# Rotary embedding of an attention block: six VectorE operations over ten heads in place of six for the keys and six for the queries

## The chip, the cores and the metric

The kernel runs on one core of one Trainium2 chip. The core has several engines that run side by side, each working through its own list of instructions in order: PE (TensorE, the matrix multiplier, whose weight loads are shown separately as PEld), DVE (VectorE), ACT (ScalarE), POOL (GpSimd) and SP (SyncE, which here only issues transfers). The metric is the device time of one execution in microseconds (us); lower is better.

## The reference, cut to what matters

The program is a two-layer encoder trunk over 2048 positions of width 1024. The change touches layer 0 only, and in it the attention half: windowed attention with 8 query heads, 2 key/value heads of 64 elements, and a rotary embedding on the first 16 elements of each query and key head.

```python
def partial_rotary(t, positions):
    half = ROPE_DIM // 2                       # ROPE_DIM = HEAD_DIM // 4 = 16
    inv_freq = jnp.power(jnp.float32(ROPE_THETA), -jnp.arange(half, dtype=jnp.float32) / half)
    ang = positions.astype(jnp.float32)[:, :, None, None] * inv_freq
    cos, sin = jnp.cos(ang), jnp.sin(ang)
    tr = t[..., :ROPE_DIM].astype(jnp.float32)
    t1, t2 = tr[..., :half], tr[..., half:]
    rot = jnp.concatenate([t1 * cos - t2 * sin, t2 * cos + t1 * sin], axis=-1)
    return jnp.concatenate([rot.astype(t.dtype), t[..., ROPE_DIM:]], axis=-1)
...
    q = partial_rotary(q.reshape(B, S, N_Q_HEADS, HEAD_DIM), positions)
    k = partial_rotary(k.reshape(B, S, N_KV_HEADS, HEAD_DIM), positions)
    y_attn = windowed_gqa_sink(q, k, v, sink)     # a block of 128 queries sees 3 blocks of 128 keys
```

Per head the rotation is four products of 8 elements, one difference and one sum. Cosine and sine depend on the position only, so that they are the same for all ten heads.

## The kernel before, in words

The sequence is cut into 16 attention blocks of 128 positions. In every tile of the attention stage the 128 positions of a block lie on the 128 partitions. The functions that matter are these.

- `build(u)` (L320) loads and transposes the input of two blocks, scales it and splits it into a high and a low part. It runs once for two blocks, so that the stage has a rhythm of block pairs.
- `project(blk)` (L344) first multiplies keys and values of the block: 24 matmuls with 256 columns into the PSUM bank `pk` (L351). Then it multiplies the queries: 24 matmuls with 512 columns into the bank `pq` (L355). The matmuls stand in the helper `mm3` (L158 to L160). ACT copies the keys (L358), the values (L361) and the queries (L362) out of PSUM; keys and queries go into one tile `qk` of ten heads, the queries in heads 0 to 7 and the keys in heads 8 and 9. Then come the rotary operations on DVE (L371 to L376), first for heads 8 to 10, then for heads 0 to 8, with the scratch tile `rot`.
- Still in `project`, the rotated keys are split for the matmul: ACT writes the high part (L380), DVE the low part (L381), PE transposes both (four transposes, L385), and ACT copies the result to its place in `kT` (L393; some blocks have two places).
- `scores(blk)` (L399) splits the rotated queries (`split`, L154 on ACT and L155 on DVE), transposes them on PE (L420), copies them (L421), multiplies them with the keys of up to three blocks (L428, L429), masks and takes the row extreme on DVE (L430), the exponential on ACT (L433), scales the rows on DVE (L440) and transposes the result in pieces of 32 by 32 on DVE (L458, two long instructions in a row). Transfers (L465) put the pieces in place.
- `values(blk)` (L469) multiplies with the values (L475) and stores the block.

The calls stand in this order: `project(0)`, `project(1)`, `scores(0)`, `project(2)`, and then for each block `blk`: `scores(blk + 1)`, for even blocks `build((blk + 4) // 2)`, `values(blk)`, `project(blk + 3)`. So `scores(n)` needs the keys of block n + 1, which are projected just ahead of it in this order. Near the end of the stage the first matmuls of the next one (the spatial gate, L549) are interleaved.

The order in which each engine runs its instructions is not written by hand. A planner places the program's instructions when the kernel is built: it steps through its own estimate of time, takes on each engine the instruction of highest priority (priority follows the order of the calls) that its estimate shows as ready, and writes that order down. On the chip every engine then follows its list in order and waits where an operand is not there yet. `qk` has four buffers, `rot` two, and the PSUM banks used for the projections (`pj`) two, for transposes (`px`) two and for the scores (`psc`) three.

Of the kernel before, what the change touches and what calls it, by code (L numbers as in the profile page):

```python
# [11 lines left out]
ALU = mybir.AluOpType  # L12
# [41 lines left out]
def kernel(  # L54
# [29 lines left out]
    tt = nc.vector.tensor_tensor  # L84
# [9 lines left out]
    def pool(stack, name, side=None, bufs=1, space=None):  # L94
        kw = {} if space is None else {"space": space}
        if side is not None:
            kw["side"] = side
        return stack.enter_context(tc.tile_pool(name=name, bufs=bufs, reuse_waits="tile", **kw))
# [58 lines left out]
    def mm3(ps, ahi, alo, bhi, blo, first, last):  # L157
        nc.tensor.matmul(ps, lhsT=ahi, rhs=bhi, start=first, stop=False)  # L158
        nc.tensor.matmul(ps, lhsT=ahi, rhs=blo, start=False, stop=False)  # L159
        nc.tensor.matmul(ps, lhsT=alo, rhs=bhi, start=False, stop=last)  # L160

    def bank(p, tag, shape=(128, C)):
        t = p.tile(list(shape), F32, tag=tag, name=tag)
        return t
# [99 lines left out]
    cos_t = ap.tile([128, 16, 8], F32, name="cos_t")  # L264
    sin_t = ap.tile([128, 16, 8], F32, name="sin_t")
# [43 lines left out]
    def k_place(n, p):  # L309
        if n not in kTs:  # L310
            kTs[n] = ap.tile([128, 4, 768], F32R, tag="kT", bufs=2, name="kT")
        return kTs[n][:, :, p * 128:p * 128 + 128]
# [31 lines left out]
    def project(blk):  # L344
        if blk >= NB:
            return
        hT = hTs[blk // 2]
        sl = slice(blk % 2 * 128, blk % 2 * 128 + 128)
        pk = bank(pj, "pj")
        for k in range(KD):  # L350
            mm3(pk[:, 0:256], hT[0][k][:, sl], hT[1][k][:, sl], wqh[:, k, 512:768], wql[:, k, 512:768], k == 0,  # L351
                k == KD - 1)
        pq = bank(pj, "pj")
        for k in range(KD):
            mm3(pq, hT[0][k][:, sl], hT[1][k][:, sl], wqh[:, k, 0:512], wql[:, k, 0:512], k == 0, k == KD - 1)  # L355
        qk = ap.tile([128, 10, 64], F32, tag="qk", bufs=4, name="qk")
        qkb[blk] = qk
        act(out=qk[:, 8:10, :], in_=pk[:, 0:128].rearrange("p (h d) -> p h d", h=2), func=AF.Copy)  # L358
        vt = ap.tile([128, 128], F32, tag="vt", bufs=7, name="vt")
        vts[blk] = vt  # L360
        act(out=vt, in_=pk[:, 128:256], func=AF.Copy)  # L361
        act(out=qk[:, 0:8, :], in_=pq.rearrange("p (h d) -> p h d", h=8), func=AF.Copy)  # L362
        rot = ap.tile([128, 4, 10, 8], F32, tag="rot", bufs=2, name="rot")
        for h0, h1 in ((8, 10), (0, 8)):
            n = h1 - h0
            cb = cos_t[:, blk:blk + 1, :].to_broadcast([128, n, 8])
            sb_ = sin_t[:, blk:blk + 1, :].to_broadcast([128, n, 8])
            t1 = qk[:, h0:h1, 0:8]
            t2 = qk[:, h0:h1, 8:16]
            r0, r1, r2, r3 = (rot[:, i, h0:h1, :] for i in range(4))  # L370
            tt(out=r0, in0=t1, in1=cb, op=ALU.mult)  # L371
            tt(out=r1, in0=t2, in1=sb_, op=ALU.mult)
            tt(out=r2, in0=t2, in1=cb, op=ALU.mult)
            tt(out=r3, in0=t1, in1=sb_, op=ALU.mult)
            tt(out=t1, in0=r0, in1=r1, op=ALU.subtract)
            tt(out=t2, in0=r2, in1=r3, op=ALU.add)  # L376
        ks = ap.tile([128, 4, 128], F32R, tag="ks", bufs=2, name="ks")
        kf = qk[:, 8:10, :]
        kd = ks[:, 0:2, :].rearrange("p k (u d) -> p k u d", u=2)
        act(out=kd, in_=kf[:, :, None, :].to_broadcast([128, 2, 2, 64]), func=AF.Copy)  # L380
        tt(out=ks[:, 2:4, :].rearrange("p k (u d) -> p k u d", u=2),  # L381
           in0=kf[:, :, None, :].to_broadcast([128, 2, 2, 64]), in1=kd.bitcast(F32), op=ALU.subtract)
        ps = bank(px, "px")
        for i in range(4):
            nc.tensor.transpose(ps[:, i * 128:i * 128 + 128].bitcast(F32R), ks[:, i, :], ident_r)  # L385
        n, p = divmod(blk, 4)
        places = [(n, p + 1)]
        if p == 0 and n > 0:
            places.insert(0, (n - 1, 5))
        if p == 3 and blk < NB - 1:  # L390
            places.append((n + 1, 0))
        for place in places:
            act(out=k_place(*place), in_=ps.rearrange("p (i n) -> p i n", i=4), func=AF.Copy)  # L393
# [108 lines left out]
    tq = pool(sb, "shuf", right)  # L502
    tail = []
    project(0)
    project(1)
    scores(0)
    project(2)
    for blk in range(NB):
        scores(blk + 1)
# [142 lines left out]
    for i in range(4):  # L652
        stt(out=bias_sg[:, i, :], in0=ps[:, i * 128:i * 128 + 128], scalar=vcol0[:, 52 + i:53 + i],
            in1=bias_sg[:, i, :], op0=ALU.mult, op1=ALU.add)
# [485 lines left out]
    op = pool(ctx, "outp", right)  # L1140
# [86 lines left out]
```

## Time and profile before

| what | value |
|---|---|
| time, median of 3 runs | 1574.51 us (1571.71 to 1579.4) |
| the profiled execution's own time | 1574.79 us |
| its span, first to last instruction | 1573.0 us |
| mean granted TensorE clock | 0.984 |
| PE busy | 1480.3 us, 94% of the span |
| PEld busy | 1184.1 us, 75% |
| DVE busy | 1187.1 us, 75% |
| ACT busy | 783.3 us, 50% |
| POOL busy | 385.2 us, 24% |
| first and last rotary operation (start) | 52.0 and 280.5 us |

How to read the rows that are quoted below. A row of the timeline has the start in us, the length in us, the engine, the line of the kernel, the operation, the tile written and the tiles read, the shape, and how many instructions are merged in the row; brackets at the end show idle time ahead of it and what ended that. A row of the groups has the number of instructions, their busy time in us, the mean of one in ns, and the idle time ahead of them. Two instructions in a row on one engine overlap a little in such rows, so that the distance between two starts says more of the cost than the length. PEclk is the share of full speed that was granted to the TensorE clock. A busy PE includes modelled ends of matmuls.

### The profile page before, as it was taken

The page shows a single profiled execution, that of the slowest core. Times are in us where ns is not written, and L with a number is a line of the kernel's source. Part 1 is how long each engine was busy: PE and PEld are TensorE (multiplying, and loading weights), DVE is VectorE, ACT ScalarE, POOL GpSimd, SP SyncE. Part 2 cuts the span into 40 slices and gives each one's busy share as a digit, 9 for nine tenths or more (in the row PEclk, how much of TensorE's full clock was granted, in tenths as well). Part 3 has the DMA queues.
Part 4 walks back from the last instruction along what each step waited for, and adds up shares of the span by engine and source line. Part 5 has one row for each costly group of instructions (what it writes and reads, how often), then busy time and mean ns, then how long its engine had stood idle before and what let it go on. Part 6 is the DMA issues. An engine that isn't in the chain of part 4 may idle for free. (4 is left out here: it accounts for less than half of the span.)

```text
span 1573.0 us, 22049 instructions
## 1 busy us (share of the span) xinstructions
PE 1480.3 (94%) x7096; PEld 1184.1 (75%) x7096; DVE 1187.1 (75%) x2180; ACT 783.3 (50%) x1470; POOL 385.2 (24%) x464
## 2 busy tenths in 40 slices
PE   6899999899999999999999899999999999868997
PEld 3787777557877777788887688788778788757886
DVE  4499889745769558966866775987987687788985
ACT  4677767543423332343243228499489496841100
POOL 1023232002004000300120232634634532133231
PEclk9999999899999999999999999999999999989999
DMA  9367776749798989988785699887877676369751
GB/s 346 124 173 217 220 199 183 236 141 297 239 291 303 253 257 293 314 272 261 263 292 180 190 262 278 239 255 281 224 243 269 220 230 221 119 198 344 253 194 54
DMA packets 210747, 370.91 MB, mean 236 GB/s; under 512 B 56616, under 2 KB 105924, under 8 KB 210632
## 3 DMA queue, kind: packets, MB, share of 16 engines
q1 hardware_dynamic: 205032, 356.89, 71.3%
q0 software_dynamic: 5600, 12.62, 3.0%
q8 instruction: 56, 0.92, 0.2%
q14 instruction: 59, 0.48, 0.1%
HBM read 261.96 MB, written 85.97 MB: 221 GB/s over the span
## 5 line engine op out<-in xcount | busy, mean ns | idle before, releaser
L154 ACT ACTIVATE hl<-raw 128x512 fp32r<-128x512 f32 x192 | 118.6, 627 | 215.4 <-DMA raw<-in_ev_w_in_dram 131.8
L159 PE MATMUL pj<-alo,hl 128*128 128x512 f32 x512 | 201.1, 393 | 0.0
L158 PE MATMUL pj<-ahi,hl 128*128 128x512 f32 x512 | 200.1, 393 | 1.1 <-DVE gz L753 1.1
L160 PE MATMUL pj<-ahi,hl 128*128 128x512 f32 x512 | 200.1, 392 | 0.0
L155 DVE TENSOR_TENSOR hl<-raw,hl 128x512 fp32r<-128x512 f32 x192 | 132.0, 698 | 63.1 <-ACT hl L154 62.7
L150 POOL TENSOR_SCALAR rstd<-mv 128x1 f32<-128x1 f32 x32 | 31.1, 972 | 415.3 <-DVE mv L616 303.6
L158 PEld LDWEIGHTS pj<-ahi,hl 128*128 128x128 f32 x512 | 96.8, 189 | 22.0 <-DVE gz L753 1.5
L159 PEld LDWEIGHTS pj<-alo,hl 128*128 128x128 f32 x512 | 96.9, 189 | 20.4
L160 PEld LDWEIGHTS pj<-ahi,hl 128*128 128x128 f32 x512 | 96.6, 189 | 20.2
L430 DVE CUSTOM_DVE_ANT_0 P<-psc,mask,nsink 128x384 f32<-128x384 f32 (+1 forms) x128 | 73.8, 596 | 24.0 <-PE psc L429 23.9
L158 PE MATMUL pj<-wqh,hhi 128*128 128x256 f32 (+1 forms) x256 | 87.9, 347 | 2.5 <-ACT hhi L154 1.7
L154 ACT ACTIVATE phl<-praw 128x512 fp32r<-128x512 f32 x56 | 35.3, 631 | 107.1 <-DMA praw<-in_od_w_in_dram 55.8
L159 PE MATMUL pj<-wql,hhi 128*128 128x256 f32 (+1 forms) x256 | 87.4, 342 | 0.0
L160 PE MATMUL pj<-wqh,hlo 128*128 128x512 f32 (+1 forms) x256 | 85.2, 345 | 1.4 <-DVE hlo L155 1.4
L977 DVE SCALAR_TENSOR_TENSOR ii<-ii,xc 128x1024 f32<-128x1024 f32 (+2 forms) x32 | 40.7, 1272 | 59.0 <-ACT ii L971 59.0
L433 ACT ACTIVATE P<-P,nm 128x384 f32<-128x384 f32 (+1 forms) x128 | 76.4, 601 | 16.4 <-DVE nm L430 15.8
L465 POOL DMA_DIRECT2D P<-T x88 | 48.8, 562 | 143.9 <-DVE nm L430 79.0
L777 POOL TENSOR_TENSOR alo<-hm,ahi 128x512 fp32r<-128x512 f32 x32 | 50.3, 1578 | 118.8 <-DVE hm L776 102.2
L947 DVE SCALAR_TENSOR_TENSOR xc<-X,vcol,xc 128x512 f32<-128x512 f32 (+2 forms) x96 | 77.7, 845 | 0.3
L158 PE MATMUL pm<-xhi,hg 128*128 128x512 f32 (+3 forms) x160 | 56.0, 364 | 14.3 <-ACT xhi L154 6.3
L155 DVE TENSOR_TENSOR phl<-praw,phl 128x512 fp32r<-128x512 f32 x56 | 39.2, 700 | 35.2 <-ACT phl L154 31.9
L966 ACT ACTIVATE ra<-pm,vcol 128x512 f32<-128x512 f32 (+2 forms) x80 | 47.2, 604 | 29.6 <-PE pm L160 29.3
(304 smaller groups left out, 4288.7 us busy)
## 6 DMA issues: line engine op xcount, KB each, us to landing
hl<-w_d SPq DMA_DIRECT2D x128, 512.0 KB, 4.8
raw<-in_ev_w_in_dram SPq DMA_DIRECT2D x128, 256.0 KB, 4.1
w_d<-phl SPq DMA_DIRECT2D x40, 512.0 KB, 4.7
aw<-in_ada_w_dram SPq DMA_DIRECT2D x32, 512.0 KB, 6.8
hg<-w_d SPq DMA_DIRECT2D x32, 512.0 KB, 4.2
P<-T SPq DMA_DIRECT2D x128, 96.0 KB, 3.8
aw<-in_ada_w_dram SPq DMA_DIRECT2D x8, 1024.0 KB, 7.7
xp<-in_x_dram SPq DMA_DIRECT2D x32, 256.0 KB, 3.3
```

Of the source, the lines that this page charges most:

```text
L154: act(out=hi, in_=src, func=AF.Copy)
L155: tt(out=lo, in0=src, in1=hi.bitcast(F32), op=ALU.subtract)
L158: nc.tensor.matmul(ps, lhsT=ahi, rhs=bhi, start=first, stop=False)
L159: nc.tensor.matmul(ps, lhsT=ahi, rhs=blo, start=False, stop=False)
L160: nc.tensor.matmul(ps, lhsT=alo, rhs=bhi, start=False, stop=last)
L430: nc.vector.tensor_tensor_reduce(out=p[:, g, 0:W], in0=ps[:, 0:W], in1=mask[:, m0:m0 + W], scale=-0.125, scalar=nsink[:, h:h + 1], op0=ALU ...
L433: act(out=p[:, g, 0:W], in_=p[:, g, 0:W], func=AF.Exp, scale=-1.0, bias=nm[:, h:h + 1], accum_out=rs[:, h:h + 1])
L465: dma.dma_start(out=pv[32 * r:32 * r + 32, 0:nb, i], in_=T[32 * i:32 * i + 32, 0:nk].rearrange("p (j r) m -> p r j m", r=4)[:, r])
L777: nc.gpsimd.tensor_tensor(out=lo[:, j], in0=h, in1=hi[:, j].bitcast(F32), op=ALU.subtract)
L947: stt(out=xc[:, w], in0=xt[:, j0 + j:j0 + j + W], scalar=vcol1[:, 8 * j + g:8 * j + g + 1], in1=xc[:, w], op0=ALU.mult, op1=ALU.add)
L966: r = act(out=ra[i][:, e, p0:p0 + n], in_=p[:, 0:n], func=AF.Sigmoid, bias=vcol1[:, 40 + q:41 + q])
L977: stt(out=ii[i][:, :, w], in0=ii[i][:, :, w], scalar=1.0, in1=xc[:, None, w].to_broadcast([128, 2, W]), op0=ALU.add, op1=ALU.mult)
```

## The change

In `project` the loop over the two groups of heads goes away. The six operations (four products, a difference, a sum) are issued once for a block, over all ten heads, where six were issued for the two key heads and six for the eight query heads. The tiles, their buffers and all else stay. The first of the six now needs both the copy of the keys (L358) and the copy of the queries (L362), and the keys are rotated by the same instructions as the queries.

```diff
         rot = ap.tile([128, 4, 10, 8], F32, tag="rot", bufs=2, name="rot")
-        for h0, h1 in ((8, 10), (0, 8)):
-            n = h1 - h0
-            cb = cos_t[:, blk:blk + 1, :].to_broadcast([128, n, 8])
-            sb_ = sin_t[:, blk:blk + 1, :].to_broadcast([128, n, 8])
-            t1 = qk[:, h0:h1, 0:8]
-            t2 = qk[:, h0:h1, 8:16]
-            r0, r1, r2, r3 = (rot[:, i, h0:h1, :] for i in range(4))
-            tt(out=r0, in0=t1, in1=cb, op=ALU.mult)
-            tt(out=r1, in0=t2, in1=sb_, op=ALU.mult)
-            tt(out=r2, in0=t2, in1=cb, op=ALU.mult)
-            tt(out=r3, in0=t1, in1=sb_, op=ALU.mult)
-            tt(out=t1, in0=r0, in1=r1, op=ALU.subtract)
-            tt(out=t2, in0=r2, in1=r3, op=ALU.add)
+        cb = cos_t[:, blk:blk + 1, :].to_broadcast([128, 10, 8])
+        sb_ = sin_t[:, blk:blk + 1, :].to_broadcast([128, 10, 8])
+        t1 = qk[:, :, 0:8]
+        t2 = qk[:, :, 8:16]
+        r0, r1, r2, r3 = (rot[:, i] for i in range(4))
+        tt(out=r0, in0=t1, in1=cb, op=ALU.mult)
+        tt(out=r1, in0=t2, in1=sb_, op=ALU.mult)
+        tt(out=r2, in0=t2, in1=cb, op=ALU.mult)
+        tt(out=r3, in0=t1, in1=sb_, op=ALU.mult)
+        tt(out=t1, in0=r0, in1=r1, op=ALU.subtract)
+        tt(out=t2, in0=r2, in1=r3, op=ALU.add)
```

## The prediction

> **What bounds the kernel now.** I read the page first, then the busy times of three stretches of the attention stage, then PE's waits there. The page names PE as the busiest engine by far.
>
> ```profile
> span 1573.0 us, 22049 instructions
> PE 1480.3 (94%) x7096; PEld 1184.1 (75%) x7096; DVE 1187.1 (75%) x2180; ACT 783.3 (50%) x1470; POOL 385.2 (24%) x464
> ```
>
> An average says little of one stage. The rotary operations start between 52.0 and 280.5 us, so the stretches that count are the steady part of the attention stage and its end. The first row below is five block pairs long, from one copy of a first block's queries (L362) to the fifth one after it; the columns are length, then busy time of each engine.
>
> ```profile
> core 0: us, PE busy (x) PEld busy (x) DVE busy (x) ACT busy (x) POOL busy (x), PEclk, DMA share, GB/s
> 97.58:262.63 165.05, 162.07 (x957) 126.79 (x956) 148.12 (x488) 122.67 (x347) 51.91 (x90) 1.00 0.72 200
> 75.00:275.00 200.00, 197.03 (x1167) 156.39 (x1166) 180.79 (x611) 148.83 (x422) 57.02 (x99) 1.00 0.70 195
> 275.00:350.00 75.00, 66.41 (x291) 43.36 (x290) 43.83 (x125) 35.07 (x92) 3.68 (x6) 0.93 0.62 186
> ```
>
> In the steady part a pair of blocks takes 165.05 / 5 = 33.0 us. PE is idle for 165.05 - 162.07 = 2.98 us of the five pairs, 0.6 us a pair. DVE is busy for 148.12 / 165.05 = 90%: high, but with 17 us of room. The waits of PE between 75 and 275 us (line that waited, releaser, us in total, times, longest) say what the little idle time is:
>
> ```profile
> PE pj L160 <- DVE hlo L155: 1.4, 1, 1.4
> PE po L475 <- issue: 0.8, 3, 0.3
> PE px L331 <- DMA xp<-in_x_dram: 0.7, 1, 0.7
> ```
>
> None waits for a rotated key or query; one of 1.4 us waits for DVE at all. The stage is bound by PE, and the operations that change stand on an engine beside it.
>
> **The change part by part.** First what goes and what grows on DVE. These are groups between 50 and 285 us, the first and the last of the six lines in both shapes (16 elements a partition for the keys, 64 for the queries); the other four lines lie between them within 7 ns.
>
> ```profile
> L371 DVE TENSOR_TENSOR rot<-qk,cos_t 128x64 f32<-128x64 f32 x16 | 3.5, 218 | 4.2 <-ACT qk L362 4.2
> L376 DVE TENSOR_TENSOR qk<-rot 128x64 f32<-128x64 f32 x16 | 3.5, 221 | 0.0
> L371 DVE TENSOR_TENSOR rot<-qk,cos_t 128x16 f32<-128x16 f32 x16 | 2.7, 171 | 2.8 <-ACT qk L358 2.8
> L376 DVE TENSOR_TENSOR qk<-rot 128x16 f32<-128x16 f32 x16 | 2.7, 170 | 0.0
> ```
>
> Next, one first block of a pair as the timeline shows it; all rows that the steps need stand here once.
>
> ```profile
> 129.41 0.17 DVE L371 TENSOR_TENSOR rot<-qk,cos_t 128x16 f32<-128x16 f32 x1
> 129.50 0.17 DVE L372 TENSOR_TENSOR rot<-qk,sin_t 128x16 f32<-128x16 f32 x1
> 129.65 0.59 ACT L362 ACTIVATE qk<-pj 128x512 f32<-128x512 f32 x1
> 130.93 0.17 DVE L376 TENSOR_TENSOR qk<-rot 128x16 f32<-128x16 f32 x1
> 131.36 3.43 DVE L458 STREAM_TRANSPOSE T<-P 128x1536 f32<-128x1536 f32 x2
> 131.93 0.41 ACT L380 ACTIVATE ks<-qk 128x256 fp32r<-128x256 f32 x1
> 135.49 0.42 DVE L381 TENSOR_TENSOR ks<-qk,ks 128x256 fp32r<-128x256 f32 x1
> 136.37 0.22 DVE L376 TENSOR_TENSOR qk<-rot 128x64 f32<-128x64 f32 x1
> 140.07 0.29 PE L385 MATMUL px<-ident_r,ks 128*128 128x128 f32 x2
> 140.40 0.60 ACT L393 ACTIVATE kT<-px 128x512 fp32r<-128x512 f32 x1 [0.55 <-PE px L385]
> 143.31 0.41 PE L428 MATMUL psc<-kT,qT 128*128 128x384 f32 x1
> ```
>
> *Removed:* 6 x 16 = 96 operations of the small shape. One costs the queue the distance of two starts, 129.50 - 129.41 = 0.09 us, so 0.54 us a block; as busy time they are 6 x 2.7 = 16.2 us.
>
> *Grown:* 96 operations go from 64 to 80 elements, a size that the trace does not show. From 16 to 64 elements one grows by (220 - 170) / 48 = 1.04 ns an element, so 16 more elements cost 17 ns: 0.10 us a block, 1.6 us in all. The lower bound is nothing, the upper one the whole small operation (0.09 us). I take 17 ns, a straight line just beyond its end.
>
> *Net on DVE:* -0.54 + 0.10 = -0.44 us a block, 16 x 0.44 = 7.0 us of queue time over the stage (by busy time 16.2 - 1.6 = 14.6 us, too much, since neighbours overlap). *Worth at the end:* PE is what sets the pace, and DVE's relief can only fill PE's idle time: at most 2.97 us between 75 and 275 us, of which 1.4 us waits for DVE. I take a gain of 0.5 us; the bounds are 0 and 3.
>
> *Moved: the keys.* Their rotation now waits for the query copy (L362), and in DVE's list it takes the place of the queries' six operations or one near it. What is queued behind: the ACT split (L380), the DVE split (L381), the four transposes (L385), the copy (L393), and the scores that use the new keys.
>
> In the first block of a pair the two copies come close together; what matters is the last of the six operations. The keys were ready at 130.93 + 0.17 = 131.10 us, and would be at 136.37 + 0.22 = 136.59 us, 5.49 us later. But L381 sat behind the two 32x32 transposes (L458) until 135.49 anyway and ended at 135.91. After the change it ends at 136.59 + 0.41 + 0.42 = 137.42, 1.51 us later. The second transposes of the keys ran at 140.07, so that 2.65 us are still in hand there; and if all behind L381 slid by the whole 1.51 us, the copy would end at 140.40 + 0.60 + 1.51 = 142.51, ahead of the scores at 143.31. Cost 0, with 0.80 us of cover in the worse reading. Without the cover each microsecond costs PE a microsecond.
>
> In the second block of the pair the query copy comes ten microseconds behind the key copy, so that the delay is large, and so is the cover:
>
> ```profile
> 139.88 0.43 DVE L381 TENSOR_TENSOR ks<-qk,ks 128x256 fp32r<-128x256 f32 x1 [0.48 <-ACT ks L380]
> 146.90 0.22 DVE L376 TENSOR_TENSOR qk<-rot 128x64 f32<-128x64 f32 x1
> 147.03 3.43 DVE L458 STREAM_TRANSPOSE T<-P 128x1536 f32<-128x1536 f32 x2
> 155.08 0.45 PE L385 MATMUL px<-ident_r,ks 128*128 128x128 f32 x4
> ```
>
> The keys would be ready at 147.12 and, even with L381 put behind the transposes, split at 147.03 + 3.43 + 0.42 = 150.88; PE takes them at 155.08. Cover 4.2 us, cost 0. The PE list loses nothing in between: the keys' transposes stood there after the queries' matmuls already.
>
> At both ends of the stage the cover is thinner:
>
> ```profile
> 62.75 0.22 DVE L376 TENSOR_TENSOR qk<-rot 128x64 f32<-128x64 f32 x1
> 66.21 0.28 PE L428 MATMUL psc<-kT,qT 128*128 128x256 f32 x1
> 280.53 0.22 DVE L376 TENSOR_TENSOR qk<-rot 128x64 f32<-128x64 f32 x1
> 281.81 3.43 DVE L458 STREAM_TRANSPOSE T<-P 128x1536 f32<-128x1536 f32 x2
> 284.39 0.34 PE L428 MATMUL psc<-kT,qT 128*128 128x384 f32 x1
> 287.43 1.19 PE L158 MATMUL pja<-hl,ahi 128*128 128x512 f32 x2 [2.52 <-DMA ahi<-h_d]
> 290.58 0.63 PE L160 MATMUL pja<-hl,alo 128*128 128x512 f32 x1
> 291.01 0.63 PE L159 MATMUL pja<-hl,ahi 128*128 128x512 f32 x1
> 293.55 0.39 PE L160 MATMUL px<-hl,alo 128*128 128x512 f32 x1
> 293.78 0.40 PE L158 MATMUL px<-hl,ahi 128*128 128x512 f32 x1
> ```
>
> At the start: 62.97 + 0.41 + 0.42 + 0.45 + 0.60 = 64.85, ahead of the first scores at 66.21. Cost 0. At the end: block 15's keys ready at 280.75, split by 281.58 if L381 goes ahead of the transposes, cost 0; if behind, 281.81 + 3.43 + 0.42 + 0.45 + 0.60 = 286.71 in place of the 284.39 at which the scores of block 14 want them. PE then waits for a transfer until 287.43 anyway, so that most of the 2.3 us is hidden. I take 0, with 2.3 as the upper bound.
>
> *Sum,* against the profiled execution's own 1574.79 us (span 1573.0, 1.8 us outside it; 0.3 us above the median of the runs shown): 1574.8 - 0.5 + 0 + 0 + 0 = 1574.3, call it **1574 us**.
>
> The rule that speaks against the change is in the Trainium skill, "Perfetto Trace Analysis", section "Optimizing Scalar/DVE Operations": grouping into larger operations pays where the engine is saturated, and where it is not but causes bubbles elsewhere, breaking instructions up may let work end sooner. At 90% DVE is between the two; by this rule the merged six would be the wrong way for the keys, which is the first rival below. By its first half the sum would be the 1568 of the second rival, by its second half the 1597 of the first. No run here shows the merged form yet; the trace of the split one shows PE without a bubble behind the keys.
>
> **The rivals.**
>
> *Slower: PE waits for the keys in each pair.* The place is the first block of a pair. If the copy of the keys slides by the whole 5.49 us (L381 behind one more burst on DVE), it ends at 141.00 + 5.49 = 146.49, 3.18 us past the scores at 143.31; 7 pairs give 22 us, 1597 us. It decides from the point where L381 ends later than 135.91 + 2.31 = 138.22. For it: the cover is under 3 us. Against: 0.80 us are left in the worse reading, and the planner can put other matmuls first. A stall can also cost twice: after the wait of 2.52 us the starts lie 0.43 us apart until 293.55, then 0.23, so PE ran at about half speed for some 6 us and lost 2.9 us more.
>
> The Trainium skill, "TensorE: Matmul & The Clock Gate", section "Why this matters for your kernels", has the clock drop after gaps over about 3 us. By that rule the stall of 3.18 us is just long enough, and by the row above shorter ones are.
>
> *Faster: DVE sets the pace after all.* PE's busy time holds modelled ends, and PEld is busy for only 126.79 / 165.05 = 77%. Then the whole relief shows: 1574.8 - 7.0 = 1568, or by busy time 1574.8 - 14.6 = 1560. Against it: PE's waits name DVE for 1.4 us in 200.
>
> *The planner writes a different order.* New estimated lengths can move ties anywhere behind the change. The work stays the same; what can move are PE's waits, 1573.0 - 1480.3 = 92.7 us over the span, the largest of them near the end of layer 1:
>
> ```profile
> PE pj L158 <- DMA wo<-wo_d: 17.6, 1, 17.6
> ```
>
> A part of one such wait, up or down, is about 10 us: 1565 or 1585.
>
> **How the numbers follow.** Forecast 0.54. Keys late 0.13, all of it slower. DVE sets the pace 0.13, of it 0.10 faster by more than 0.5%. Another order 0.20: 0.08 faster, 0.07 slower, 0.05 neither. 0.5% is 7.9 us, about what a measurement of this kernel can tell from no change. So faster 0.18, within 0.54 + 0.03 + 0.05 = 0.62, slower 0.20. The likeliest case's own range is 1570 to 1579 (gain to 3, loss to 2.3, and the spread of the runs shown). The range for 8 in 10 goes to 1562, inside the faster rival, and to 1588, between the replanned order and the rival with late keys; beyond lie about 0.08 on either side.
>
> **What the profile after would show.** Right: 96 rotary operations of about 237 ns and none of the small shape; a pair still 33 us long with PE idle for about 0.6 us of it; DVE busy some 14 us less between 50 and 285 us; L381 later, L385 and L428 at their old distances. Wrong: waits of PE (L385, L428) on L381 or on the copy L393, pairs 2 us longer and a lower granted clock (slower rival); pairs shorter by 1 us with DVE as full as before (faster rival); equal pairs but waits moved behind 350 us (another order). A rotary operation over 100 ns longer than I take it would break the sum on DVE.

## The result, and the profile after

The kernel after takes 1586.83 us, median of 4 runs (1584.96 to 1588.39), against 1573.43 us, median of 4 runs of the kernel before in the same comparison. The ratio is 1.0068, 95% interval 1.0047 to 1.0089: slower by 13.4 us. The forecast was 1574.0 us, no change.

The page of the profiled execution after (1584.96 us): the span and the busy time of each engine.

```profile
span 1583.3 us, 21941 instructions
PE 1488.5 (94%) x7096; PEld 1185.2 (75%) x7096; DVE 1179.2 (74%) x2084; ACT 784.9 (50%) x1470; POOL 388.6 (25%) x464
```

The span has grown by 10.3 us. DVE lost 96 instructions and 1187.1 - 1179.2 = 7.9 us of busy time, close to the 7.0 us of queue time that the prediction took off. The groups of the kernel after (mean length of one in ns) show the new size near the estimate of 237 ns:

```profile
L369 DVE TENSOR_TENSOR rot<-qk,cos_t 128x80 f32<-128x80 f32 x16 | 3.8, 235 | 14.0 <-ACT qk L362 14.0
...
L374 DVE TENSOR_TENSOR qk<-rot 128x80 f32<-128x80 f32 x16 | 3.7, 231 | 0.0
```

So the change does on DVE what it says. The time is lost elsewhere. The start of each block's query copy (L362) tells where, read from the timelines of both kernels:

| query copy of block | 0 | 2 | 3 | 4 | 6 | 8 | 10 | 12 | 14 | 15 |
|---|---|---|---|---|---|---|---|---|---|---|
| before, us | 52.04 | 71.45 | 85.69 | 97.58 | 129.65 | 162.42 | 195.74 | 227.13 | 262.63 | 276.31 |
| after, us | 51.69 | 69.98 | 80.89 | 101.19 | 139.35 | 171.75 | 203.56 | 237.46 | 274.61 | 289.42 |
| later by | -0.4 | -1.5 | -4.8 | 3.6 | 9.7 | 9.3 | 7.8 | 10.3 | 12.0 | 13.1 |

Almost all of it is lost once, between blocks 3 and 6; from there to block 12 a pair takes (237.46 - 139.35) / 3 = 32.7 us, where it took (227.13 - 129.65) / 3 = 32.5 us. Another 2.8 us go between blocks 12 and 15. The busy times by stretch, first of the kernel before, then of the one after (length, then busy time of each engine, the granted clock behind the engines):

```profile
75.00:100.00 25.00, 25.00 (x160) 22.63 (x158) 23.11 (x86) 21.30 (x63) 4.38 (x8) 1.00 0.56 170
100.00:125.00 25.00, 24.71 (x143) 18.49 (x142) 23.36 (x78) 19.06 (x53) 10.51 (x18) 1.00 0.66 182
125.00:150.00 25.00, 25.00 (x147) 19.09 (x146) 21.75 (x73) 17.01 (x49) 5.55 (x10) 1.00 0.69 188
...
150.00:250.00 100.00, 98.67 (x583) 76.97 (x581) 89.11 (x299) 74.71 (x211) 30.96 (x55) 1.00 0.75 209
```

```profile
75.00:100.00 25.00, 22.21 (x137) 18.92 (x136) 21.11 (x74) 21.25 (x64) 4.52 (x8) 1.00 0.40 121
100.00:125.00 25.00, 21.87 (x117) 15.96 (x117) 19.06 (x62) 17.91 (x54) 5.30 (x9) 0.89 0.58 164
125.00:150.00 25.00, 25.00 (x144) 19.31 (x141) 21.51 (x62) 13.80 (x40) 10.06 (x17) 0.97 0.66 189
...
150.00:250.00 100.00, 98.47 (x584) 76.42 (x583) 84.57 (x250) 73.40 (x203) 30.21 (x53) 1.00 0.71 203
```

Between 75 and 150 us PE was busy for 74.71 us before and is for 69.08 us after: 5.6 us more idle time. The clock takes up to 25 x 0.11 + 25 x 0.03 = 3.5 us more, an estimate from above, since it also counts a low clock while PE was idle. Together that is up to 9.1 us, near the 9.7 by which block 6 is late. From 150 to 250 us the two kernels are alike.

What PE waits for in that stretch of the kernel after (line, releaser, us in total, times, longest):

```profile
PE px L331 <- ACT P L431: 3.0, 1, 3.0
PE px L331 <- DMA xp<-in_x_dram: 1.6, 1, 1.6
PE pj L158 <- ACT hhi L154: 0.6, 1, 0.6
```

No row names a key. PE's longest waits stand ahead of the transposes of the next block pair's input (`build`, L331). The timeline of the kernel after shows how the start has moved; matmuls of the projections between these rows are left out.

```profile
60.91 0.60 ACT L362 ACTIVATE qk<-pj 128x512 f32<-128x512 f32 x1 [0.85 <-PE pj L160]
...
61.54 0.24 DVE L369 TENSOR_TENSOR rot<-qk,cos_t 128x80 f32<-128x80 f32 x1 [5.96 <-ACT qk L362]
...
63.21 0.43 DVE L379 TENSOR_TENSOR ks<-qk,ks 128x256 fp32r<-128x256 f32 x1 [0.54 <-ACT ks L378]
...
67.69 0.46 PE L383 MATMUL px<-ident_r,ks 128*128 128x128 f32 x4
...
71.88 0.35 PE L426 MATMUL psc<-kT,qT 128*128 128x256 f32 x1
...
108.01 1.94 PE L473 MATMUL po<-P,vt 128*64 128x512 f32 x8
...
115.13 0.60 PE L331 MATMUL px<-ident,xp 128*128 128x128 f32 x4
...
116.11 6.00 SPq L325 DMA_DIRECT2D xp<-in_x_dram  x3
...
120.62 1.09 PE L331 MATMUL px<-ident,xp 128*128 128x128 f32 x4 [3.00 <-ACT P L431]
...
122.28 4.84 PE L473 MATMUL po<-P,vt 128*64 128x512 f32 x12
```

Block 1's keys wait for the query copy at 60.91, are split at 63.64, and PE takes them only at 67.69, without a wait of its own: its list has projection matmuls ahead of them. In the kernel before the same two steps were:

```profile
57.27 0.43 DVE L381 TENSOR_TENSOR ks<-qk,ks 128x256 fp32r<-128x256 f32 x1 [0.84 <-ACT ks L380]
...
61.12 0.45 PE L385 MATMUL px<-ident_r,ks 128*128 128x128 f32 x4
```

There the transposes stood 61.12 - 57.70 = 3.42 us behind the split; in the kernel after it is 67.69 - 63.64 = 4.05 us. The distance went along with the keys. It did so in first blocks of a pair, too: in block 6 the last transposes stood 4.16 us behind the split and stand 4.03 us behind it. In second blocks it did not: there the distance was long, 13.8 us in block 5 and 14.8 us in block 7, and shrank to 3.3 and 1.4 us.

The first scores are 5.67 us late (71.88 for 66.21). PE does projections ahead in the meantime (block 3's query copy is 4.8 us early), and I take it that what it has done ahead it lacks later. The first values come at 108.01 in place of 100.68. At 120.62 PE resumes after 3.00 us of waiting. The row names ACT, but these transposes read no `P`. What they need, I take it, is a load that could be issued only once the transposes at 115.13 had freed one of two input buffers, at 115.73; it was issued at 116.11, and loads in this stretch landed 3.8 us after their issue, at about 120. In the kernel before, twelve value matmuls (113.60 us) stand in PE's list between two such groups of transposes (111.49 and 116.78 us); here they stand behind the wait, at 122.28.

### The profile page after: what moved, and what is told of

Its sections match the earlier page's. It is cut to its first block, busy times and chain, and to the rows that moved or that the text cites. A ratio compares the mean times of both kernels' runs of the same rounds, so it can differ in the third digit from the quotient of the medians.

```text
span 1583.3 us, 21941 instructions
## 1 busy us (share of the span) xinstructions
PE 1488.5 (94%) x7096; PEld 1185.2 (75%) x7096; DVE 1179.2 (74%) x2084; ACT 784.9 (50%) x1470; POOL 388.6 (25%) x464
## 5 line engine op out<-in xcount | busy, mean ns | idle before, releaser
L158 PE MATMUL pj<-wqh,hhi 128*128 128x512 f32 (+1 forms) x256 | 87.6, 346 | 3.1 <-ACT hhi L154 2.3
L159 PE MATMUL pj<-wql,hhi 128*128 128x512 f32 (+1 forms) x256 | 87.2, 341 | 0.0
L775 POOL TENSOR_TENSOR alo<-hm,ahi 128x512 fp32r<-128x512 f32 x32 | 49.7, 1562 | 117.9 <-DVE hm L774 113.9
```

What stands on the lines that cost most here:

```text
L775: nc.gpsimd.tensor_tensor(out=lo[:, j], in0=h, in1=hi[:, j].bitcast(F32), op=ALU.subtract)
```

## The experiments

Two theories were told apart first. One: the keys' wait for the query copy costs the time, wherever it comes from. The other: what decides is the count and size of DVE's operations, or simply that the planner wrote another order. Ratios are to the kernel before, measured side by side, with 95% intervals.

**The wait and the operations, one without the other.** Four kernels. The first keeps twelve operations a block, but puts one query head into the keys' group, so that the keys need the query copy:

```diff
-        for h0, h1 in ((8, 10), (0, 8)):
+        for h0, h1 in ((7, 10), (0, 7)):
```

> Twelve operations in two groups as before, but the first group is heads 7 to 10 and the second heads 0 to 7: elements and number of operations stay, and the keys now need the query copy, as after. Theory 'start' and rival 'every pair' both: the wait for the query copy is the cause, 1582 to 1590 us. If the merged operation itself (its size, or six fewer instructions in the planner's estimate) were the cause, this would be at 1572 to 1577 us.

The second has six operations a block and no wait: keys apart, three operations for a group over all 16 rotated elements of a head, with tables of cosine and signed sine made once by four small POOL operations (`cb` and `sb_` are 16 wide here, `r1v` is `r1` in two halves). It was measured twice.

```diff
+        for h0, h1 in ((8, 10), (0, 8)):
...
+            t = qk[:, h0:h1, 0:16]
+            tt(out=r0, in0=t, in1=cb, op=ALU.mult)
+            tt(out=r1, in0=t, in1=sb_, op=ALU.mult)
+            tt(out=t.rearrange("p h (u d) -> p h u d", u=2), in0=r0.rearrange("p h (u d) -> p h u d", u=2),
+               in1=r1v[:, :, ::-1, :], op=ALU.add)
```

> Keys first and queries after them as before, but each group in three operations over 16 elements a head (product with cosine twice over, product with sine of both signs, sum with the halves exchanged): six operations a block as after, without the wait for the query copy. Four small POOL operations are added once to lay out the tables. Theories 'start' and 'every pair': no loss, 1570 to 1575 us; relief of DVE brings at most 1 to 3 us since PE sets the pace. If fewer operations were harmful in themselves: 1580 us or more.

> The kernel with the keys apart and three operations of 16 elements a head for each group, once more and with more rounds: six operations a block, as in the kernel after, and no wait of the keys for the query copy. Theory that late keys cost the time: 0.994 to 0.999 of before, as the first time. Theory that each new order of the planner is a draw of plus or minus 0.4% and the first result was a lucky one: the same order gives the same time, so that this can only tell whether 0.997 was noise of the measurement; then 0.999 to 1.002.

The last has the same three operations over all ten heads, three a block, with the wait:

```diff
-        for h0, h1 in ((8, 10), (0, 8)):
+        for h0, h1 in ((0, 10),):
```

> The same three operations, but over all ten heads, so three operations a block and keys that wait for the query copy: the fewest operations of all kernels here. Theory that the count of operations on VectorE sets the time: at most 0.997. Theory that late keys cost the time: 1.003 to 1.008, although DVE has the least to do.

| kernel | operations a block | keys wait | ratio |
|---|---|---|---|
| before | 12 | no | 1 |
| one query head with the keys | 12 | yes | 1.0118 (1.0077 to 1.0160) |
| after | 6 | yes | 1.0068 (1.0047 to 1.0089) |
| three operations a group | 6 | no | 0.9970 (0.9946 to 0.9994), again 0.9977 (0.9957 to 0.9996) |
| three operations, all heads | 3 | yes | 1.0077 (1.0056 to 1.0098) |

The wait alone makes the kernel slower by 1.2% (1594.82 us, above the 1582 to 1590 expected), and with the three operations it is the whole difference between 0.9977 and 1.0077. With early keys half as many operations buy 0.2 to 0.3%, and once the keys are late a second halving buys nothing. By wait is meant here that the keys' operations name the query copy as an input: the planner sees it too and writes another order, and these runs don't part the two. Groups of the two kernels with three operations, the one without the wait first (its line numbers are 377 to 379):

```profile
L377 DVE TENSOR_TENSOR rot<-qk,cos 128x128 f32<-128x128 f32 x16 | 4.6, 286 | 4.9 <-ACT qk L368 4.8
...
L377 DVE TENSOR_TENSOR rot<-qk,cos 128x32 f32<-128x32 f32 x16 | 3.0, 186 | 3.3 <-ACT qk L364 3.2
```

```profile
L377 DVE TENSOR_TENSOR rot<-qk,cos 128x160 f32<-128x160 f32 x16 | 5.1, 321 | 20.9 <-ACT qk L368 20.9
```

DVE has the least to do in the merged one, but it stands idle for 20.9 us ahead of the first operation, where it was 4.9 + 3.3 us. Their stretch from 75 to 150 us, without the wait and then with it:

```profile
75.00:150.00 75.00, 73.56 (x439) 59.35 (x439) 66.53 (x206) 58.55 (x164) 20.02 (x35) 1.00 0.65 183
```

```profile
75.00:150.00 75.00, 68.76 (x408) 55.17 (x407) 61.25 (x184) 53.54 (x159) 20.31 (x35) 1.00 0.60 170
```

PE is busy for 73.56 - 68.76 = 4.8 us less with the wait, much as in the kernel after (5.6 us). The kernel with keys apart and three operations beats both kernels: before by 0.2 to 0.3%, after by about 1%.

**Where the loss is made.** Five kernels use the merged form for some blocks and the split form for the others; the first one, split for blocks 0 to 2, stands for all:

```diff
-        cb = cos_t[:, blk:blk + 1, :].to_broadcast([128, 10, 8])
+        for h0, h1 in ((8, 10), (0, 8)) if blk < 3 else ((0, 10),):
```

> Blocks 0 to 2 are rotated in two groups (keys first) as before, blocks 3 to 15 in one group as after. Theory 'start': the loss is made where the first scores wait for the keys of block 1 (first score matmul at 66.21 us before, 71.88 us after); it comes back here, so 1573 to 1577 us, and the first score matmul at about 66 us. Rival 'every pair': 13 of 16 blocks still have late keys, so about 1583 to 1587 us. Rival 'another order': neither; any time between 1570 and 1590, with waits in places that neither names.

> The reverse: blocks 0 to 2 in one group as after, blocks 3 to 15 in two groups as before. Theory 'start': nearly the whole loss, 1582 to 1588 us, first score matmul at about 72 us. Rival 'every pair': three blocks of sixteen, 1574 to 1577 us. The two kernels together should add up to the whole loss of 13 us if either theory holds; if they do not, the order that the planner writes has a share of its own.

> Two groups in blocks 0 to 7, one group from block 8 on. Theory 'slip': the query copies of blocks 0 to 7 at the times of before, a loss of about 10 us within the two pairs after block 8, 1583 to 1590 us. Rival 'start only': 1573 to 1578 us. Rival 'a cost for each late block': about 1580 us.

> One group in the even blocks only, the first of each pair, whose key and query copies lie 0.9 us apart in the trace of before. Theory 'slip by the wait for the query copy': little to lose, 1572 to 1580 us. If the order that the planner writes suffers from any merged block: 1585 us or more.

> One group in the odd blocks only, the second of each pair, whose query copy lies 6 to 11 us behind the key copy (from 104.02 to 110.28 us, from 133.33 to 143.22). Theory 'slip': the whole loss, 1583 to 1592 us, with PE idle and a lower granted clock between 75 and 150 us. If the 4.2 us of cover that the prediction counted there were real: 1573 to 1578 us.

| merged in | ratio | query copy later than before, at block 4, 6, 8, 10, 14 (us) |
|---|---|---|
| blocks 3 to 15 | 1.0061 (1.0041 to 1.0081) | -1.0, 4.8, 8.7, 9.0, 9.3 |
| blocks 0 to 2 | 1.0086 (1.0056 to 1.0117) | 3.8, 8.4, 8.7, 8.4, 8.4 |
| blocks 8 to 15 | 1.0090 (1.0069 to 1.0110) | -0.3, -0.2, -0.2, 10.3, 18.9 |
| even blocks | 1.0113 (1.0087 to 1.0140) | 5.1, 5.0, 13.6, 17.9, 26.6 |
| odd blocks | 1.0073 (1.0047 to 1.0099) | 5.8, 8.8, 6.7, 10.6, 14.9 |

This struck down the thought that the thin cover at the start was the only cause: with the start split again some 9 us are lost all the same, about a pair further on. The first two kernels lose 0.61% and 0.86%, together about twice the 0.68% of the change, so that, as their expectation has it, the order that the planner writes has a share of its own. It struck down a cost for each late block, too: three merged blocks cost as much as sixteen. In the first three kernels of the table the loss is a slip, made within some blocks behind the point where keys turn from early to late. With three merged blocks the copy of block 6 stands at 138.07 us and that of block 14 at 271.07, exactly the 133.0 us of the kernel before: thirteen blocks with early keys behind it give nothing back, since PE has next to no idle time in which to catch up (98.49 of the 100 us from 150 to 250 us are busy).

The lateness of a copy shows where time goes in one traced execution, and not what the kernel loses as a whole: two kernels below, with early keys and another order (priority on the keys' chain), stand 6.1 and 8.0 us late at block 14, and their ratios are 1.0026 and 1.0004. (Their traced executions took 1584.54 and 1580.40 us, above their medians of 1578.76 and 1577.22.)

Even blocks alone, whose query copy comes about a microsecond behind the key copy, cost more than odd ones. Their expectation gave them little to lose if the length of that wait set the price, and 1585 us or more if any merged block upset the order; they took 1595.47 us, so the length of the wait doesn't set the price. Nor does the number of turns from early to late keys: both kernels turn late in each pair, and cost less than the kernel below whose pairs alternate (1.0200, four turns). Both also hold a block of the start (0, or 1), so that neither tries its place in the pair by itself.

In the kernel that turns late at block 8 the slip is seen directly. Its timeline, first the row of PE, then SP's issues ahead of it:

```profile
181.23 0.66 PE L331 MATMUL px<-ident,xp 128*128 128x128 f32 x4
...
197.32 1.09 PE L331 MATMUL px<-ident,xp 128*128 128x128 f32 x4 [6.42 <-DMA xp<-in_x_dram]
```

```profile
178.60 0.38 SPq L325 DMA_DIRECT2D xp<-in_x_dram  x1
...
181.69 7.45 SPq L465 DMA_DIRECT2D P<-T  x8
...
193.07 5.73 SPq L325 DMA_DIRECT2D xp<-in_x_dram  x3
```

The transposes at 181.23 had freed a buffer at 181.89, but the next loads of `build` stand in SP's list behind eight transfers of `P` and five stores, until 193.07: eleven microseconds with a free buffer and no load. PE is idle for 6.42 us.

**Is it the late loads?** The largest loss came where pairs of blocks alternate between the two forms, and its waits of PE between 75 and 350 us are mostly for input loads:

```diff
+        for h0, h1 in ((0, 10),) if blk // 2 % 2 == 1 else ((8, 10), (0, 8)):
```

> Blocks 2, 3, 6, 7, 10, 11, 14, 15 in one group, the others in two: the keys turn late four times. Theory 'slip' (PE loses its lead once, each time that the keys turn from early to late, some 10 us, and a saturated PE never gets it back): more than the change itself, 1595 to 1615 us. Rival 'a cost for each late block': half the loss of the change, about 1580 us. Rival 'one slip for all': like the change, 1585 to 1590 us.

```profile
PE px L331 <- DMA xp<-in_x_dram: 16.9, 9, 4.4
```

Two ways to free the loads were tried on it, each with a control on the kernel before: issue them on ACT, which has no eight transfers in its list, or give `xp` a third buffer, so that they can be issued earlier.

```diff
-            load(out=xp, in_=xs[u * 256:u * 256 + 256, k2 * 256:k2 * 256 + 256].rearrange("(b p) f -> p b f", p=128))
+            nc.scalar.dma_start(out=xp, in_=xs[u * 256:u * 256 + 256, k2 * 256:k2 * 256 + 256].rearrange("(b p) f -> p b f", p=128))
```

```diff
-            xp = jp.tile([128, 2, 256], F32, tag="xp", bufs=2, name="xp")
+            xp = jp.tile([128, 2, 256], F32, tag="xp", bufs=3, name="xp")
```

> The alternating kernel (keys late in blocks 2, 3, 6, 7, 10, 11, 14, 15; 31 us over before), with the input loads of build (L325) issued from ACT's list in place of SP's. Theory 'load behind the transfers': PE's waits there are for input loads that the planner put behind eight transposed pieces (L465, some 0.9 us of issue each) in SP's list; with the loads out of that list most of the loss goes, 1575 to 1590 us, and no wait of PE on xp over 1 us. Rival 'keys': PE waits because the scores come late, whatever the load does; 1600 us or more, with waits under another name.

> Control: the kernel before with its input loads issued from ACT's list. Both theories: within 5 us of before, 1572 to 1582 us, since before has only 0.7 us of waits for these loads between 75 and 275 us; a load that waits for PE can hold ACT's list up, which would add some us.

> The alternating kernel with three buffers in place of two for the input tile of build, loads on SP as before, so that a load need not wait for PE to free the tile before. Theory 'load behind the transfers': part of the loss goes, 1580 to 1600 us. Rival 'keys': 1603 to 1612 us as with two buffers.

> The kernel before with a third buffer for the input of the block pairs: the control of the two runs with three such buffers (alternating 1.0047, after 1.0088). Theory that late loads behind the transfers make the alternating kernel's extra loss: the control stands at 0.998 to 1.002, so that the alternating kernel has kept only what late keys cost once. Theory that the buffer merely moves the planner's order: the control differs from 1 by more than 0.003, and nothing follows from those two runs.

> The kernel after with three buffers for the input tile. Theory 'load behind the transfers': the wait of 3.0 us near 120 us and the one of 2.4 us near 258 us shrink, 1575 to 1583 us. Rival 'keys': 1584 to 1590 us.

| input loads | keys early | pairs alternate | all late (kernel after) |
|---|---|---|---|
| on SP, two buffers | 1 | 1.0200 (1.0182 to 1.0218) | 1.0068 |
| on ACT, two buffers | 1.0109 (1.0076 to 1.0141) | 1.0153 (1.0118 to 1.0187) | - |
| on SP, three buffers | 1.0040 (1.0021 to 1.0059) | 1.0047 (1.0024 to 1.0071) | 1.0088 (1.0058 to 1.0117) |

Both means make the kernel before slower by themselves, so the columns are read across a row. Loads on ACT decide nothing: the alternating kernel still waits 14.5 us for input loads (16.9 us with loads on SP; no wait over 1 us was expected, and the longest is 3.4 us), and its 1599.91 us lie just under the 1600 of the rival, far from the 1575 to 1590 of the theory. That it stands only 1.0153 / 1.0109 = 1.004 over its control owes much to the control's own loss.

The third buffer does free the loads: in the alternating kernel PE's waits for them fall from 16.9 to 0.8 us between 75 and 350 us, and the loss falls from 2.0% to 1.0047 / 1.0040 = 1.001 over its control. By the expectation for that control, one off by more than 0.003 meant that nothing follows; it is off by 0.004, and I read the run with that caution. For the kernel after, the buffer doesn't carry the case: 1.0088 / 1.0040 = 1.005 is left, close to its 1.0068. So late loads are likely most of the alternating kernel's loss, but not the 10 us of the kernel after: with the third buffer the wait of 3.00 us is gone (the longest left between 75 and 150 us is 1.4 us) and the loss is not. I take it that there the wait for the input is the place where PE's missing work shows, and not its cause.

**Is it the planner's place for the keys?** PE took the keys 4.05 us after they were split. So the rotary operations and the whole chain of the keys, down to the copies to `kT`, were put at high priority, with controls:

```diff
+        with tc.high_priority():
             rot = ap.tile([128, 4, 10, 8], F32, tag="rot", bufs=2, name="rot")
...
```

> The kernel after, with the whole of the rotary operations and the keys' chain behind them (both splits, the four transposes, the copy to kT) placed at high priority, so that the planner writes them down as soon as its estimate shows them ready. Theory that the loss lies in the place that the planner gives the keys' chain (it starts the four transposes 4.05 us behind the DVE split in block 1): most of the loss goes, at most 1.003 of before, first scores at about 67 us. Theory that the wait of the data for the query copy is what costs, wherever the chain is placed: 1.005 to 1.009, as without it.

> The same priority on the kernel before: what the priority is worth by itself, without any wait of the keys. Both theories: 0.996 to 1.003 of before. The run ahead of this one is read against it.

> The same priority on the kernel with the keys apart and three operations for a group. Theory of the planner's place: keys that are early in the data and in the list leave PE waiting least, 0.993 to 0.998 of before. Theory of the data alone: as without the priority, 0.995 to 0.999.

After: 1.0080 (1.0051 to 1.0109). Before: 1.0026 (0.9999 to 1.0053). Three operations: 1.0004 (0.9986 to 1.0023), above both expectations. The loss stays: 1.0080 / 1.0026 = 1.0054 for late keys. The timeline of the kernel after with priority says why this could not help:

```profile
64.16 0.43 DVE L380 TENSOR_TENSOR ks<-qk,ks 128x256 fp32r<-128x256 f32 x1 [0.54 <-ACT ks L379]
```

```profile
68.65 0.46 PE L384 MATMUL px<-ident_r,ks 128*128 128x128 f32 x4
```

The transposes still come 68.65 - 64.59 = 4.06 us behind the split. The priority did not move them, so that the theory of the planner's place is not tried by this run. Priority chooses among what the planner's estimate holds for ready; I take it that by this estimate the keys weren't ready sooner. That is argued: the estimates stand in no trace. The two controls also show what an order of the planner's is worth by itself, where no key is late: three operations went from 0.997 to 1.000, the kernel before to 1.003.

**What stays open.** How the 9 us of the kernel after divide: up to 3.5 of them are a lower clock, the rest is PE without work, and whether late scores or late loads took that work away isn't shown. Whether late keys cost by the data on the chip or by the order that the planner then writes: no run holds the order fixed. And whether an order written out by hand, with late keys and loads in good places, would lose nothing: it wasn't tried.

## Why the prediction was wrong

*Right: the terms on DVE.* The operation of 80 elements took 231 to 235 ns (237 taken), DVE's busy time fell by 7.9 us over the span (7.0 of queue time taken), and the 14.6 us were rightly called too much.

*Right: PE bounds the stage, so that a relief of DVE is worth little.* Six operations a block without the wait gave 0.2 to 0.3%, some 4 us, more than the 0.5 us taken; the intervals reach from about 1 to 8 us, so that the bound of 3 is neither kept nor broken. DVE doesn't set the pace: with late keys, three operations a block gained nothing over six.

*Wrong: "cost 0" for the moved keys.* This step failed, at the start (blocks 0 to 2 alone: 1.0086) and in the steady part (late from block 8 on: 1.0090); the end of the stage wasn't tried by itself. It held the distance from the keys to their user in the old trace (64.85 against 66.21 at the start, 0.80 to 2.65 us in first blocks, 4.2 us in second ones) for slack that would take up the delay. The data came when the sum said: the split at the start was to end at 62.97 + 0.41 + 0.42 = 63.80 and ended at 63.64. But the transposes, taken to follow at once, came 4.05 us later, and the scores 5.67 us later than before. In their place PE lost up to 9.1 us between 75 and 150 us, 5.6 us of it idle, and never got them back. The short distances, of some 4 us at the start and in first blocks, moved along with the keys; I take them for places in lists that the planner writes with its own estimate of the keys' chain in mind. The row that could have warned was in the trace of before: there, too, PE took the split keys 3.42 us late, without a wait. In second blocks the distance did give way, from 13.8 and 14.8 us to 3.3 and 1.4 us, and the pairs behind the slip run at 32.7 us (32.5 before): there, behind the slip, the cover did take the delay up.

*Wrong: that each microsecond of an uncovered stall costs PE a microsecond in each pair, or nothing.* The loss is neither per pair nor zero: in the kernel after it is paid nearly all at once, and three late blocks cost as much as sixteen. What sets its size isn't shown: kernels that turn late several times cost between 0.7% (odd blocks) and 2.0% (alternating pairs). The rival with late keys in each pair had the right cause, and a wrong size (1597 us) and place: pairs behind the slip stayed at 32.7 us, and no wait of PE between 75 and 150 us names a key. The rival of another order named 1585 us, near the measured time, but for ties moved by new lengths: new orders with early keys lie between 0.997 and 1.003 where only priority or the operations changed (moved loads and a third buffer cost 1.0109 and 1.0040), all but one of the kernels with late keys between 1.006 and 1.020, and that one (1.0047) is level with its own control. That 1586.83 us still lies inside the range of 1562 to 1588 us is luck: its upper end was set by these two rivals.

*The signs named for "wrong"* were waits of PE on L381 or L393, pairs 2 us longer with a lower clock, shorter pairs, or waits moved behind 350 us. Of these the lower clock came (0.89 from 100 to 125 us), and one pair 6 us longer (from block 4 to block 6, 38.2 us for 32.1), but no wait on the keys. Here the dependency, which the planner knows about, doesn't show as a wait at its place; it shows as missing work a pair or two later.

*The clock.* It did cost twice: behind the 3.00 us wait at 120.62 us the twelve value matmuls took 4.84 us, where such a row took 2.79 us in the kernel before:

```profile
113.60 2.79 PE L475 MATMUL po<-P,vt 128*64 128x512 f32 x12 [0.23 <-issue]
```

The Trainium skill, "TensorE: Matmul & The Clock Gate", section "Why this matters for your kernels", names idle gaps of over about 3 us for the drop. The traces here don't show such an edge: in the kernel after with three input buffers the clock was 0.50 from 97 to 100 us, behind two waits of 1.03 and 0.59 us, and in the merged kernel with three operations it stayed at 1.00 around a wait of 2.63 us (at 120.72 us).

*The rule on grouping.* The Trainium skill, "Perfetto Trace Analysis", section "Optimizing Scalar/DVE Operations", would group operations where the engine is saturated and break them up where they cause bubbles elsewhere. The runs are in keeping with both halves: grouping the elements of a head gained 0.2 to 0.3%, grouping keys with queries lost 0.7%. What decided here is that the second kind of grouping also joins two dependencies: with the operations kept at twelve, the joined dependency alone lost 1.2%.

## What to carry to other kernels

Merge operations whose inputs arrive together (the two halves of a head), not operations that join an early input with a late one (keys with queries), even on an engine that is 90% busy. In a program whose order a planner writes, the distance between a result and its user in the old trace need not be slack: here distances of 4 us moved along with the result, and distances of 14 us shrank. Put a price on the delay unless a run shows that it is taken up, and look for it as missing work later as well as for a wait at the place. On an engine that is busy to 98%, a slip made once was kept to the end of the stage, so that a change that touches three blocks cost as much as one that touches sixteen.

## What the hardware showed beside this

The length of a rotary operation (float32 TENSOR_TENSOR) on DVE and 128 partitions is a straight line in its elements over ten times the range: 170 ns at 16, 186 at 32, 220 at 64, 233 at 80, 286 at 128 and 321 at 160, about 1.04 ns an element. Eight transfers of `P` issued in a row occupy SP's list for 7.45 us in the kernel that turns late at block 8 (0.66 us at the median, 1.77 us the longest), so that a load behind them is late by that much. Moving the loads to ACT was no cure: the kernel before became 1.1% slower, with PE waiting up to 6.1 us for a load.
